# A Mamba-2 and pooling block on one core: where the later adaLN product-sums stand, and in which order the first weights are cast

## The chip, the core and the metric

The kernel runs on one core of a Trainium2 chip. The time is the device time in microseconds (us) of one execution. The engines are TensorE (PE in the profile, with PEld for its weight loads), VectorE (DVE), ScalarE (ACT), GpSimd (POOL) and SyncE (SP), which here issues nearly all transfers. Each engine works its own instructions off in order and waits on semaphores for the others.

## What is computed

One decoder block for 512 tokens of width 1024, in float32. A vector `c` gives six rows of 1024 numbers (shift, scale and gate of each of two sub-layers), and these modulate everything else:

```
mod = silu(c) @ w_ada + b_ada            # 6 x 1024 numbers
shift_m, scale_m, gate_m, shift_f, scale_f, gate_f = split(mod, 6)
h = rmsnorm(x, norm_mix_w) * (1 + scale_m) + shift_m
z, xbc, dt, u_pool, gate_logits = split(h @ w_in)
y = scan(silu(conv(xbc)), dt) * silu(z)          # Mamba-2, 4 groups of 8 heads
y_ssd  = rmsnorm(y by group) @ w_branch_ssd
y_pool = pool(u_pool) @ w_branch_pool
x = x + gate_m * ((sig(g0) * y_ssd + sig(g1) * y_pool) @ w_out)
h = rmsnorm(x, norm_mlp_w) * (1 + scale_f) + shift_f
x = x + gate_f * (relu(h @ w_up) ** 2 @ w_down)
out = rmsnorm(x, norm_final_w)
```

`mod` is held as 48 columns of 128 numbers: columns 0 to 7 shift_m, 8 to 15 scale_m, 16 to 23 gate_m, 24 to 31 shift_f, 32 to 39 scale_f, 40 to 47 gate_f.

## The kernel before

**Three matmuls for one.** PE multiplies in a rounded float format. To keep float32 precision each operand is split into a high part (a cast on ACT) and a low part (the rest, a subtraction on DVE), and each product is three matmuls: high by high, high by low, low by high (`mm3`, L155 to L157). `split` (L125 cast, L126 subtraction) does this for data.

**Units.** A unit is 128 output rows of a weight matrix by all 512 tokens, 24 matmuls. `load_unit` brings its 512 KB weight block: SP issues the transfer into one of four raw buffers (`RAW`, L140), ACT casts it (L145), DVE subtracts (L146), into two of eight `HL` tiles, so that four units' weights can stand ready. The raw buffer is free again after the subtraction, the `HL` tiles after the unit's last matmul. Each of these pools is handed out in turn, in the order in which the program asks.

**The product-sums.** A column of `mod` isn't made on PE. `ada(j)` takes a raw buffer, SP loads a 512 KB block of the transposed `w_ada` into it (L170), and one DVE instruction multiplies it by the row silu(c) and sums (L171). There are 48. Sixteen (shift_m and scale_m) are needed for the first operand and stand in the first stage. The other 32 are spread over later stages: after each of the eight units of the pooling gate (columns 16 to 23), after each of the eight pooling-branch units (24 to 31), after each of the eight units of the other gate (32 to 39), and eight in the first five units of the output projection (40 to 47).

**The order.** The stages are: the first input units with the modulation of the first operand; the remaining z units of group 0; four groups of the state-space scan; gate units; pooling-branch units; second gate units; output projection and the norm; up and down projections. In the first stage the order of each engine is the program's own (`tc.manual_schedule()`). After it a planner orders each engine's instructions: it plays the program through with estimated durations and gives each engine, whenever it is free, the earliest instruction in the program of those that are ready; weight loads rank ahead of all (`urgent`).

**The first stage.** For each of eight slices `k` of the contraction: DVE makes `t` (L305), ACT adds the shift and writes the operand's high part (L306), DVE its low part (L310). The weights of slice 0 come in two transfers, 256 columns (L274 casts them) and the rest (issued at L293, cast at L308); L278 subtracts for all. L320 are the matmuls of seven units, slice by slice; L314 those of the step sizes.

**A group of the scan** (`ssd_group`) works on four chunks of 128 tokens. `prepare(c)` loads decay rows (`cs_d`, L482), masks them on POOL (L487), takes exponentials on ACT (L491), multiplies on DVE (L492), transposes x on PE (L495), and scales it by the step size (L497); for the first three chunks it also scales by the decay on POOL (L503) and splits that for the state's matmul. A chunk then computes the state (three matmuls of `mm3`), the old state's share (L521), and the chunk's own (L541). `run(g, fillers)` gives the program alternately a step of group g and some units of PE work: units of the next group (B, C, four x, four z units: `u_z`, whose result goes to `sz` at L431), or the branch units (`bs`) of the group before. L578 is the norm's sum at a group's end.

**The output projection** does five of its eight units whole, and units 5 to 7 in two halves of 256 tokens each. `residual` (L751) adds a unit to x, squares it (L758), sums the squares (L759), and `norm` (L768) adds them up over the partitions, once for each half. The `wup` blocks of the next stage are loaded meanwhile (L974, L976) and split by `two` (L828, L829).

Of the kernel before, what the change touches and what calls it, by code (L numbers as in the profile page):

```python
# [9 lines left out]
AF = mybir.ActivationFunctionType  # L10
# [52 lines left out]
def block_kernel(tc, xp, crow, arow, par, adaT, wstart, wz, wx, wpool_in, wgate, wpw, wbs, wbp, wout, wup, wdn, out):  # L63
# [3 lines left out]
    with (  # L67
# [99 lines left out]
        def ada(j, at=RAW):  # L167
# [3 lines left out]
            dve.tensor_tensor_reduce(r, r, cbc, 1.0, col("b_ada", j), ALU.mult, ALU.add, mod[:, j:j + 1])  # L171
            at.put(r)

        def column_sums(ps, sqs, c0, c1, opened=False):

            if len(sqs) == 1 and not opened:
                for c in range(c0, c1):
                    pe.matmul(ps[:, c:c + 1], sqs[0][:, c * P:(c + 1) * P], ones[:, :1], start=True, stop=True)
                return
            if not opened:  # L180
                pe.matmul(ps[:, c0:c1], ones, zeros[:, c0:c1], start=True, stop=False)
            for i, sq in enumerate(sqs):
                for c in range(c0, c1):
                    pe.matmul(ps[:, c:c + 1], sq[:, c * P:(c + 1) * P], ones[:, :1], start=False,
                              stop=i == len(sqs) - 1 and c == c1 - 1)
# [32 lines left out]
        with tc.manual_schedule():  # L218
            raw0 = RAW.get()
            crow_t = raw0[:1]  # L220
            act.dma_start(crow_t, crow)
            mt = [MT.get() for _ in range(3)]
            xs1 = HL.get()
            xpair = [m.rearrange("p h k -> p (h k)") for m in mt] + [xs1]
            xs0 = [xpair[k // 2][:, k % 2 * T:k % 2 * T + T] for k in range(8)]
            for i in range(4):
                sp.dma_start(xpair[i], xp[i])
            sp.dma_start(par_t, par)
            warm(12)
            wide = HL.get()  # L230
            dve.memset(wide, 0.0)
            act.activation(wide[:1], crow_t, AF.Silu)
            cps = [PU.get(), PU.get()]
            for i in range(2):
                pe.matmul(cps[i], ones, wide[:, i * T:(i + 1) * T], start=True, stop=True)
            HL.put(wide)
            ps = PU.get()
            sq = [HL.get() for _ in range(4)]

            def halves(i):  # L240
                dve.tensor_tensor(sq[i][:, :T], sq[i][:, :T], sq[i][:, T:], ALU.add)

            def sums(i):
                pe.matmul(ps, ones, sq[i][:, :T], start=i == 1, stop=i == 3)

            for i in range(3):
                act.activation(sq[i], xpair[i], AF.Square)
                halves(i)
                if i == 1:
                    dve.tensor_tensor(sq[1][:, :T], sq[1][:, :T], sq[0][:, :T], ALU.add)  # L250
            act.copy(cbc[:, :T], cps[0])
            act.activation(sq[3][:, :T], xpair[3][:, :T], AF.Square)
            act.copy(cbc[:, T:], cps[1])
            act.preload_act_table_set("natural_log_exp_and_others")
            dve.tensor_tensor(sq[3][:, T:], xpair[3][:, T:], xpair[3][:, T:], ALU.mult)
            halves(3)
            for i in range(1, 4):
                sums(i)
            warm(5)
            PU.put(*cps)  # L260
            RAW.put(raw0)
            HL.put(*sq)

            def scale(k):
                act.activation(amod[:, k:k + 1], mod[:, 8 + k:9 + k], AF.Identity,
                               bias=col("nmix", k), scale=col("nmix", k))

            W0 = NU * P + NH

            def begin(k, n=W0):  # L270

                r, hi, lo = RAW.get(), HL.get(F32R), HL.get(F32R)
                sp.dma_start(r[:, :n], wstart[k][:, :n])
                act.copy(hi[:, :n], r[:, :n])  # L274
                return r, hi, lo

            def end(r, hi, lo):
                dve.tensor_tensor(lo[:, :W0], r[:, :W0], hi[:, :W0].bitcast(F32), ALU.subtract)  # L278
                pool.tensor_copy(hi[:, W0:W0 + NH], lo[:, W0 - NH:W0].bitcast(F32))
                RAW.put(r)  # L280
                HL.put(hi, lo)
                return [(hi[:, o:o + n], lo[:, o:o + n]) for o, n in [(NU * P, 2 * NH)] + [(o, P) for o in range(0, NU * P, P)]]

            h = []
            ada(8, EARLY)
            w = begin(0, 2 * P)
            R = S.get()
            act.activation(R, ps, AF.Ln, bias=eps_t, scale=1.0 / DM)
            act.activation(R, R, AF.Exp, scale=-0.5)
            PU.put(ps)  # L290
            dve.tensor_scalar(amod[:, :1], mod[:, 8:9], 1.0, col("nmix"), ALU.add, ALU.mult)
            ada(0, EARLY)
            sp.dma_start(w[0][:, 2 * P:W0], wstart[0][:, 2 * P:])  # L293
            first = [PS.get() for _ in range(8 - NPU)] + [PU.get() for _ in range(NPU)]
            for k in range(8):
                hi, lo = S.get(F32R), S.get(F32R)
                h.append((hi, lo))
                t = S.get()
                shift = mod[:, k:k + 1]
                if k:  # L300
                    w = begin(k)
                    ada(8 + k, EARLY)
                    scale(k)
                    ada(k, EARLY)
                dve.scalar_tensor_tensor(t, xs0[k], amod[:, k:k + 1], R, ALU.mult, ALU.mult)  # L305
                act.activation(hi, t, AF.Identity, bias=shift)  # L306
                if k == 0:
                    act.copy(w[1][:, 2 * P:W0], w[0][:, 2 * P:W0])  # L308
                w = end(*w)
                dve.scalar_tensor_tensor(lo, t, shift, hi.bitcast(F32), ALU.add, ALU.subtract)  # L310
                S.put(t)
                def dt_unit():
                    for i in range(2):
                        pe.matmul(first[0][:2 * NH], w[0][0], h[k][i], start=k == 0 and i == 0, stop=k == 7 and i == 1)  # L314

                for i in range(3):
                    if k == 7 and i == 2:
                        dt_unit()
                    for u in range(1, NU + 1):
                        pe.matmul(first[u], w[u][i // 2], h[k][i % 2], start=k == 0 and i == 0, stop=k == 7 and i == 2)  # L320
                if k < 7:
                    dt_unit()
            sp.dma_start(ea, arow[0:1, :].broadcast_to([P, NH]))
            act.activation(ea, ea, AF.Exp)
# [101 lines left out]
        def u_z(g, i):  # L426
            def f():
                if "sz" not in G[g]:
                    G[g]["sz"] = SZ.get()
                ps = unit(wz[4 * g + i], h)  # L430
                with tc.issue_after(act.activation(G[g]["sz"][:, i, :], ps, AF.Silu).ins):  # L431
                    silus()
                PU.put(ps)
            return f

        acc = [None] * 8
# [20 lines left out]
        def ssd_group(g):  # L457
# [20 lines left out]
            def prepare(c):  # L478
# [22 lines left out]
                if c < 3:  # L501
                    t = S.get()
                    pool.tensor_tensor(  # L503
                        v3(t), v3(xdt), decg[:, c, :].unsqueeze(2).broadcast_to([P, HG, 64]), ALU.mult)
                    xd = split(t)
                    S.put(t)
                return m, xdt, xd

            ready = [prepare(0)]
            yield  # L510
            for c in range(NC):
                cc = slice(c * P, (c + 1) * P)
                if c < NC - 1:
                    ready.append(prepare(c + 1))
                    yield
                m, xdt, xd = ready.pop(0)
                yo = None
                if c > 0:
                    yo = PS.get()
# [172 lines left out]
        for j in range(8):  # L692
            gp = F.get()
            ps = unit(wgate[8 + j], h)
            behind(act.activation(gp, ps, AF.Sigmoid))
            PU.put(ps)
            merged.append(gp)
            if j == 1:
                for _ in rest:
                    pass  # L700
                later.append(SZ.get())
                F.free += range(12, 16)
                PU.free += PS.free
            if j == 3:
                for i in range(4):
                    bs(3, i)()
                pool_mix(1)()
            ada(16 + j)
        for j in range(8):
            ps = unit(wbp[j], pout)  # L710
            dve.tensor_tensor(merged[j], merged[j], ps, ALU.mult)
            PU.put(ps)
            ada(24 + j)
        free(pout)
        mg = []
        for j in range(8):
# [7 lines left out]
            F.put(merged[j])  # L724
            mg.append(split(gs))
            F.put(gs)
            with tc.issue_after(done[0].ins):
                ada(32 + j)
        free(h)
        with tc.issue_after(last.ins):  # L730
            table = act.preload_act_table_set("natural_log_exp_and_others")
# [42 lines left out]
        for j in range(5):  # L774
            ps = unit(wout[j], mg)
            residual(ps, j, 16)
            PU.put(ps)
            ada(40 + j)
            if j > 1:
                ada(43 + j)  # L780
        for k in range(8):
            dve.tensor_scalar(
                amod[:, 8 + k:9 + k], mod[:, 32 + k:33 + k], 1.0, col("nmlp", k), ALU.add, ALU.mult)
# [405 lines left out]
```

## Time and profile before

| | us |
|---|---|
| median of 3 runs | 967.26 (966.17 to 967.54) |
| profiled execution | 968.35 |
| its span, first to last instruction | 966.6 |

The windows view splits the span. These are busy us in each stretch, and what the transfers moved:

| stretch | what runs there | PE | DVE | ACT | GB/s |
|---|---|---|---|---|---|
| 0 to 60 | first input units | 54.77 | 48.59 | 30.83 | 295 |
| 60 to 132 | group 0 | 71.38 | 61.65 | 65.31 | 144 |
| 132 to 312 | groups 1 and 2 | 179.77 | 123.93 | 110.82 | 114 |
| 312 to 426 | group 3 | 114.00 | 88.34 | 56.80 | 113 |
| 426 to 560 | gate, branch, second gate units | 134.00 | 81.96 | 43.96 | 175 |
| 560 to 624 | end of those, output projection, norm | 61.19 | 52.10 | 28.11 | 203 |
| 624 to 966.6 | up and down projections, end | 334.83 | 202.46 | 163.34 | 91 |

The row of groups 1 and 2 adds two stretches of the view. A busy PE isn't a PE at its peak, as matmuls overlap; what tells is the time in which it stands idle, and what it waits for.

### The profile page before, as it was taken

How to read it: one execution, taken by the hardware profiler on the slowest of the kernel's cores; microseconds unless marked ns; L12 is line 12 of the kernel's file. 1: busy time of each engine (PE TensorE's matmuls, PEld its weight loads, DVE VectorE, ACT ScalarE, POOL GpSimd, SP SyncE). 2: the span in 40 equal slices, each digit the busy share in tenths (PEclk: the TensorE clock that was granted, in tenths of full speed). 3: DMA queues.
4: the chain of work that ended last, by engine and by line, in shares of the span. 5: the costliest groups of instructions: out<-in, count | busy, mean ns of one | idle time of the engine just before them, and what ended most of it. 6: DMA issues, size and time to landing. Idle time of an engine off the chain costs nothing.

```text
span 966.6 us, 13246 instructions
## 1 busy us (share of the span) xinstructions
PE 949.9 (98%) x5131; PEld 803.6 (83%) x5131; DVE 659.0 (68%) x961; ACT 499.2 (52%) x811; POOL 89.7 (9%) x91
## 2 busy tenths in 40 slices
PE   7999999999999999999999999999999999999996
PEld 4877888888888888888888888998899889889986
DVE  7978869467866787978533897895557556664533
ACT  5479975667528542663312334684157127425632
POOL 0102321220312132300000000000000000000000
PEclk9999999999999999999999999999999999999999
DMA  9746333433253334338632687442144225214002
GB/s 369 293 134 178 121 111 120 131 110 109 77 157 110 101 102 131 131 101 254 211 106 90 214 273 241 140 146 69 52 142 132 66 74 166 88 33 153 23 1 87
DMA packets 61761, 129.22 MB, mean 134 GB/s; under 512 B 4673, under 2 KB 29505, under 8 KB 61698
## 3 DMA queue, kind: packets, MB, share of 16 engines
q1 hardware_dynamic: 61696, 128.38, 41.6%
q8 instruction: 40, 0.66, 0.3%
q14 instruction: 23, 0.19, 0.1%
q10 hardware_dynamic: 2, 0.00, 0.0%
HBM read 126.13 MB, written 2.23 MB: 133 GB/s over the span
## 4 chain that ended last, share of the span: by engine, by line
PE 86%; DVE 5%; DMA 4%; ACT 2%; issue 1%; POOL 0%; SPq 0%; DVEq 0%; ACTq 0%; POOLq 0%
PE ps L155 22%; PE ps L156 22%; PE ps L157 22%; PE ps L887 12%; PE ps L320 4%; DMA d<-cs_d 2%; PE ps L541 2%; DMA d<-wout 1%; PE ps L521 1%; DVE d L171 1%; DMA d<-wstart 1%; DVE d L146 1%; DVE s L389 1%; PE ps L495 1%; DMA d<-wup 1%
## 5 line engine op out<-in xcount | busy, mean ns | idle before, releaser
L155 PE MATMUL ps<-s,d 128*128 128x512 f32 (+1 forms) x1080 | 412.2, 382 | 1.8 <-ACT d L145 1.0
L156 PE MATMUL ps<-s,d 128*128 128x512 f32 (+1 forms) x1080 | 408.1, 378 | 0.0
L157 PE MATMUL ps<-s,d 128*128 128x512 f32 (+1 forms) x1080 | 408.1, 378 | 0.0
L155 PEld LDWEIGHTS ps<-s,d 128*128 128x128 f32 x1080 | 202.7, 188 | 42.7 <-issue 2.4
L157 PEld LDWEIGHTS ps<-s,d 128*128 128x128 f32 x1080 | 202.7, 188 | 38.5 <-DVE d L146 0.3
L156 PEld LDWEIGHTS ps<-s,d 128*128 128x128 f32 x1080 | 202.9, 188 | 37.0 <-DVE s L126 0.2
L145 ACT CAST d<-d 128x1024 fp32r<-128x1024 f32 x88 | 92.0, 1046 | 126.6 <-PE ps L156 109.5
L146 DVE TENSOR_TENSOR d<-d,d 128x1024 fp32r<-128x1024 f32 x88 | 112.6, 1280 | 65.6 <-ACT d L145 60.8
L887 PE MATMUL ps<-s,d 128*128 128x256 f32 x864 | 103.8, 279 | 0.0
L887 PEld LDWEIGHTS ps<-s,d 128*128 128x128 f32 x864 | 102.9, 188 | 0.2
L828 ACT CAST d<-d 128x1024 fp32r<-128x1024 f32 x44 | 45.8, 1049 | 79.3 <-PE ps L156 62.8
L1076 DVE SCALAR_TENSOR_TENSOR xs<-ps,mod,xs 128x512 f32<-128x512 f32 x29 | 21.7, 750 | 69.7 <-PE ps L157 69.7
L828 ACT CAST d<-sz 128x1024 fp32r<-128x1024 f32 x32 | 33.7, 1052 | 68.8 <-PE ps L156 48.9
L829 DVE TENSOR_TENSOR d<-d,d 128x1024 fp32r<-128x1024 f32 x44 | 53.5, 1223 | 22.3 <-ACT d L828 20.8
L829 DVE TENSOR_TENSOR d<-sz,d 128x1024 fp32r<-128x1024 f32 x32 | 39.2, 1224 | 19.8 <-ACT d L828 16.5
L171 DVE CUSTOM_DVE_ANT_0 d<-d,d,par_t 128x1024 f32<-128x1024 f32 x32 | 41.6, 1305 | 8.2 <-DMA d<-adaT 8.2
L320 PE MATMUL ps<-s,d 128*128 128x512 f32 x168 | 40.7, 394 | 2.3 <-ACT s L306 1.9
L491 ACT ACTIVATE d<-d,ncs 128x128 f32<-128x128 f32 x128 | 39.9, 391 | 3.6 <-POOL d L487 3.6
L320 PEld LDWEIGHTS ps<-s,d 128*128 128x128 f32 x168 | 31.2, 188 | 10.9 <-ACT s L306 2.8
L389 DVE SCALAR_TENSOR_TENSOR s<-ps,par_t,s 128x511 f32<-128x511 f32 (+2 forms) x54 | 39.6, 740 | 0.3
L125 ACT CAST s<-s 128x512 fp32r<-128x512 f32 x32 | 19.7, 619 | 23.8 <-POOL s L503 18.7
L126 DVE TENSOR_TENSOR s<-s,s 128x512 fp32r<-128x512 f32 x32 | 27.4, 858 | 4.5 <-ACT s L125 4.5
(219 smaller groups left out, 1000.0 us busy)
## 6 DMA issues: line engine op xcount, KB each, us to landing
d<-adaT SPq DMA_DIRECT2D x32, 512.0 KB, 4.2
d<-wx SPq DMA_DIRECT2D x18, 512.0 KB, 3.6
d<-wdn SPq DMA_DIRECT2D x18, 512.0 KB, 4.0
d<-cs_d SPq DMA_DIRECT2D x16, 512.0 KB, 6.1
d<-wbs SPq DMA_DIRECT2D x16, 512.0 KB, 3.5
d<-wgate SPq DMA_DIRECT2D x16, 512.0 KB, 3.6
d<-wz SPq DMA_DIRECT2D x15, 512.0 KB, 3.5
sz<-wdn SPq DMA_DIRECT2D x14, 512.0 KB, 4.0
```

The lines of the kernel that those rows point to most:

```text
L145: act.copy(hi[:, :w], r[:, a:a + w])
L146: (low or dve).tensor_tensor(lo[:, :w], r[:, a:a + w], hi[:, :w].bitcast(F32), ALU.subtract)
L155: pe.matmul(ps, whi, xhi[:, t0:t1], start=start, stop=False)
L156: pe.matmul(ps, whi, xlo[:, t0:t1], start=False, stop=False)
L157: pe.matmul(ps, wlo, xhi[:, t0:t1], start=False, stop=stop)
L171: dve.tensor_tensor_reduce(r, r, cbc, 1.0, col("b_ada", j), ALU.mult, ALU.add, mod[:, j:j + 1])
L320: pe.matmul(first[u], w[u][i // 2], h[k][i % 2], start=k == 0 and i == 0, stop=k == 7 and i == 2)
L389: dve.scalar_tensor_tensor(t[:, sh:], ps[:, :T - sh], w(3 - sh), t[:, sh:], ALU.mult, ALU.add)
L491: act.activation(m[:, i, :], m[:, i, :], AF.Exp, bias=ncs[:, c, g * HG + i:g * HG + i + 1])
L828: act.copy(dst[0], src)
L829: dve.tensor_tensor(dst[1], src, dst[0].bitcast(F32), ALU.subtract)
L887: pe.matmul(ps, x, y, start=start and m == 0 and i == 0, stop=m == 3 and i == 2, skip_group_check=True)
```

## The change

1. `ada_next` hands out the 32 later product-sums in order, columns 16 to 47. One follows each z unit of groups 1 to 3 (12; these units run as fillers of groups 0 to 2), one each of the eight pooling-gate units and the four branch units `bs(3, i)` among them (12), and one each of the eight pooling-branch units (8). The second gate units and the output projection have none.
2. In slice 0 of the first stage, ACT casts the rest of the first weights before it writes the operand's high part, not after.
3. The split of the decay-scaled x leaves `prepare(c)`. It is asked for at the beginning of chunk c, ahead of `prepare(c + 1)`.

```diff
+        rows = list(range(16, 48))
+
+        def ada_next(n=1):
+
+            for _ in range(n):
+                ada(rows.pop(0))
...
                 dve.scalar_tensor_tensor(t, xs0[k], amod[:, k:k + 1], R, ALU.mult, ALU.mult)
-                act.activation(hi, t, AF.Identity, bias=shift)
                 if k == 0:
                     act.copy(w[1][:, 2 * P:W0], w[0][:, 2 * P:W0])
+                act.activation(hi, t, AF.Identity, bias=shift)
...
                 with tc.issue_after(act.activation(G[g]["sz"][:, i, :], ps, AF.Silu).ins):
                     silus()
                 PU.put(ps)
+                if g:
+                    ada_next()
...
-                    xd = split(t)
-                    S.put(t)
+                    xd = t
                 return m, xdt, xd
...
                 cc = slice(c * P, (c + 1) * P)
+                m, xdt, xd = ready.pop(0)
                 if c < NC - 1:
+                    t, xd = xd, split(xd)
+                    S.put(t)
                     ready.append(prepare(c + 1))
                     yield
-                m, xdt, xd = ready.pop(0)
...
+            ada_next()
             if j == 3:
                 for i in range(4):
                     bs(3, i)()
+                    ada_next()
                 pool_mix(1)()
-            ada(16 + j)
...
             PU.put(ps)
-            ada(24 + j)
+            if rows:
+                ada_next()
...
-            with tc.issue_after(done[0].ins):
-                ada(32 + j)
...
             residual(ps, j, 16)
             PU.put(ps)
-            ada(40 + j)
-            if j > 1:
-                ada(43 + j)
```

## The prediction

> **What bounds the kernel now.** I read the page first.
>
> ```profile
> span 966.6 us, 13246 instructions
> PE 949.9 (98%) x5131; PEld 803.6 (83%) x5131; DVE 659.0 (68%) x961; ACT 499.2 (52%) x811; POOL 89.7 (9%) x91
> ```
>
> TensorE (PE) is busy for 98% of the span and its matmuls don't change. So only the places where PE stands still can be won or lost. The view of waits, for PE alone, lists them (waited-for instruction, us in total, times, longest):
>
> ```profile
> PE ps L320 <- ACT s L306: 1.9, 1, 1.9
> PE ps L768 <- DVE sz L759: 1.6, 1, 1.6
> ...
> PE ps L155 <- ACT d L145: 1.0, 1, 1.0
> ...
> PE ps L155 <- ACT sz L431: 0.4, 1, 0.4
> PE ps L320 <- DVE s L310: 0.4, 1, 0.4
> PE ps L578 <- DVE s L126: 0.2, 1, 0.2
> ```
>
> The L320 waits are in the first input units. L145 and L768 are at the output projection, where later product-sums now sit. L431 and L578 are the only waits in the state-space groups. The view by windows gives the engines' load in the stretches of groups 0, 1 and 2 (columns: stretch, its length, busy us of PE, PE weight load, DVE, ACT, POOL, then clock, DMA share, GB/s):
>
> ```profile
> 60.00:132.00 72.00, 71.38 (x381) 57.39 (x380) 61.65 (x105) 65.31 (x124) 19.36 (x19) 1.00 0.47 144
> 132.00:222.00 90.00, 89.77 (x463) 73.59 (x462) 60.54 (x86) 59.87 (x111) 18.47 (x19) 1.00 0.39 114
> 222.00:312.00 90.00, 90.00 (x466) 74.24 (x465) 63.39 (x93) 50.95 (x91) 17.44 (x17) 1.00 0.39 114
> ```
>
> VectorE (DVE) has 10.35 us free in the first (72.00 less 61.65), 29.5 in the second, 26.6 in the third. The clock is full.
>
> **Part 1, the first weights.** From the timeline of the start, and one piece of the chain of waits (the DMA of the first weights' rest):
>
> ```profile
> 4.87 7.60 DMA d<-wstart
> ```
>
> ```profile
> 14.36 0.72 ACT L306 ACTIVATE s<-s,mod 128x512 fp32r<-128x512 f32 x1 [0.82 <-DVE s L305]
> 14.98 0.74 ACT L308 CAST d<-d 128x672 fp32r<-128x672 f32 x1
> 15.13 2.08 PE L320 MATMUL ps<-s,d 128*128 128x512 f32 x7 [1.90 <-ACT s L306]
> 15.76 1.12 DVE L278 TENSOR_TENSOR d<-d,d 128x928 fp32r<-128x928 f32 x1 [1.44 <-ACT d L308]
> 16.80 0.74 DVE L310 SCALAR_TENSOR_TENSOR s<-s,mod,s 128x512 fp32r<-128x512 f32 x1
> 17.60 3.45 PE L320 MATMUL ps<-s,d 128*128 128x512 f32 x14 [0.39 <-DVE s L310]
> 20.65 0.73 ACT L306 ACTIVATE s<-s,mod 128x512 fp32r<-128x512 f32 x1 [1.48 <-DVE s L305]
> 21.43 2.83 PE L320 MATMUL ps<-s,d 128*128 128x512 f32 x11
> ```
>
> The rest has landed at 12.47, and ScalarE (ACT) stands idle for 0.82 us before L306 at 14.36. The cast L308 (0.74) fits into that gap: 13.54 to 14.28, so L306 isn't pushed back. L278 then starts when DVE is done with L305, at 14.3 instead of 15.76, and L310 ends near 16.1 instead of 17.54. PE has all its high weights at 15.13, does its 7 matmuls without a break at some 0.24 us each (3.45 over 14) until 16.75, and goes on at once where it now goes on at 17.60: **-0.85 us**. It lasts if the next operand comes as much earlier. That one (L306 at 20.65) ends with DVE's work, which moves by 1.4, and needs two more rows:
>
> ```profile
> 7.10 1.61 SPq L170 DMA_DIRECT2D xs<-adaT  x2
> ```
>
> ```profile
> xs<-adaT SPq DMA_DIRECT2D x8, 512.0 KB, 7.8
> ```
>
> Issued by 8.7 and 7.8 us to landing, the second operand of its product-sums is there near 16.5, before DVE gets to it (16.1 plus one product-sum). So the next operand is ready near 20.0, and PE, done at 20.6, doesn't wait. Bounds: 0 if one of these transfers is later, -0.9.
>
> **Part 2, what goes away at the output projection.** The chain of waits there (start, us, what):
>
> ```profile
> 578.89 1.14 DVE d L171
> 580.13 5.80 DMA d<-wout
> 585.95 1.05 ACT d L145
> ...
> 599.74 5.05 DMA d<-wup
> 604.82 1.06 ACT d L828
> 605.90 1.23 DVE d L829
> 607.46 0.41 DVE xs L751
> 607.88 0.42 ACT sz L758
> 608.33 0.44 DVE sz L759
> 608.81 0.71 PE ps L768 x2
> ```
>
> A product-sum (L171) gives its raw buffer back, only then is `wout`'s block issued, it lands 5.8 us later, and its cast L145 is what PE waited 1.0 us for. After the change no product-sum stands between these loads: a load waits for the subtraction four loads earlier, which lies some 20 us back. **-1.0**; bounds 0 and -1.0.
>
> The second wait has the same root. The sum for the norm (L751, L758, L759, then L768) runs 607.46 to 608.81, 1.35 us. L751 stood behind L829 on DVE, and that behind a `wup` block which landed at 604.8. When could it have started? The window from 596.75 to 606.85 shows
>
> ```profile
> 596.75:606.85 10.10, 10.10 (x85) 10.06 (x85) 7.74 (x12) 5.35 (x8) 0.00 (x0) 1.00 0.77 238
> ```
>
> 85 matmuls: 72 are the first halves of units 5 to 7 (three units of 24), one is the end of the unit before, 12 are of the second halves, put ahead of the norm. At 10.10/85 = 0.12 each these 12 take 1.4 us, so unit 7 was ready near 605.4 and the norm's matmul could start at 606.9, when PE ran dry. With `wup` loaded earlier DVE is free at 605.4 and the 1.6 us go, all but 0.1: **-1.5**. Bounds: 0 if another thing is in DVE's way, -1.6. What is late next: the norm's own chain, which the 12 matmuls just cover.
>
> **Part 3, what the groups take on.** Twelve product-sums go into the z units of groups 1 to 3, which run during groups 0 to 2, four in each. Each is one 512 KB transfer on SP's queue, one of four raw buffers, and one DVE instruction. The rows of that line, DVE's wait for it, and one case beside GpSimd (POOL):
>
> ```profile
> L171 DVE CUSTOM_DVE_ANT_0 d<-d,d,par_t x32: 1253/1280/2089, 379.2 to 592.0; 128x1024 f32<-128x1024 f32 x32
> ```
>
> ```profile
> DVE d L171 <- DMA d<-adaT: 8.2, 9, 2.0
> ```
>
> ```profile
> 394.86 1.06 POOL L623 TENSOR_TENSOR pad<-pad 128x527 f32<-128x527 f32 x1 [2.84 <-DVE s L627]
> ```
>
> Four in a stretch are 5.1 us of DVE (4 times 1.28): they fit into 29.5 and 26.6 with ease, into group 0's 10.35 just. The dearest one took 2.09, and the POOL addition at 394.86 ran in that time. The Trainium skill (SBUF — State Buffer, Who interferes with whom) says that a VectorE instruction with both inputs in SBUF and a GpSimd instruction that reads SBUF shut each other out; the trace agrees by that one case, and by this rule four of them would cost group 0 up to 3.2 us more of DVE, still inside its free time.
>
> While a product-sum waits for its transfer (2.0 at the longest), what stands behind it on DVE waits too: weight subtractions, convolutions, the scan's operands; PE reads those. Weights are up to four units ahead of PE (eight tiles, two each). The scan is nearer: in group 0
>
> ```profile
> 111.92 0.94 DVE L126 TENSOR_TENSOR s<-s,s 128x512 fp32r<-128x512 f32 x1
> ```
>
> ```profile
> 113.89 0.48 PE L155 MATMUL ps<-s,s 128*128 128x512 f32 x1
> ```
>
> the state operand's low part ended at 112.86, only 1.03 us before PE took it. On SP's queue a transfer that waits for its raw buffer holds up the decay rows (`cs_d`) and other weights behind it. Bounds: -0.6 (the L431 and L578 waits vanish) to 5.1 (group 0's four all on PE's path). The nearest row is the waits view, where all groups cost PE 0.6 with DVE at 86% in group 0; I double it: **+0.6**.
>
> The moved split (ACT cast, DVE subtraction; same count) removes ACT's stops behind POOL:
>
> ```profile
> ACT s L125 <- POOL s L503: 18.7, 7, 4.1
> ```
>
> No PE wait hangs on these, so 0. In exchange the operand is made one filler later; if the 1.03 us above are used up, it costs what is missing, a subtraction (0.94) or so; this lies inside the bound.
>
> The gate stage's twelve (eight before) and the eight in the branch units stay at 0. The window of the gate, branch and second gate units up to 560 shows PE without a gap beside the sums there now, and DVE with a third of its time free:
>
> ```profile
> 426.00:560.00 134.00, 134.00 (x593) 111.00 (x592) 81.96 (x111) 43.96 (x55) 0.00 (x0) 1.00 0.55 175
> ```
>
> **The sum.** -0.85 - 1.0 - 1.5 + 0.6 = -2.75. The profiled execution took 968.35 (span 966.6, 1.75 around it), which would become 965.6; it is 1.1 above the median of the runs, 967.26, and from the median the sum gives **964.5**. About 0.2%, 1.9 us, is what a measurement of this kernel can tell from no change.
>
> **The rivals.** *The norm still waits*: DVE is held by other `wup` subtractions, or the planner puts fewer matmuls ahead of the norm. For it: wait and chain are only 1.4 us apart. Against: the chain names the late transfer. -0.85 - 1.0 + 0.6 = -1.25, 966.0; no measurable change.
>
> *It doesn't do what it says*: the planner, which orders by buffer and readiness, lets the sums drift back to where the raw buffers are free, as it drew three of the gate stage's forward (their line starts at 379.2, before that stage). Then only part 1 is left: 966.4.
>
> *Group 0 becomes the bound*, which makes it slower: four product-sums stand in DVE's queue ahead of the scan's operands. Priced with the dearest row, 4 times 2.09 = 8.4 on PE's path instead of 0.6: -3.35 + 8.4 = +5.0, 972.3. It decides from the point where a sum and its wait take more than the 1.03 us of slack before L155 in group 0; a sum alone is 1.28. For it: DVE at 86% and ACT at 91% there. Against: later chunks of groups 1 and 2 show no PE wait, and a late sum's order is below the scan's own work.
>
> **How the numbers follow.** Forecast 0.55, the norm still waits 0.19, drift 0.09, group 0 bound 0.17. The first is faster by over 0.2%, the next two lie within, the last is slower. The low end takes every bound at its best: -0.9 - 1.0 - 1.6 - 0.6 = -4.1, and 0.6 for small waits beside these: 962.5. The high end takes in the first two rivals and the mild part of the third, 967.9; what is left out is most of the third.
>
> **What would show it.** Part 1: the second L320 row starts near 16.75 and PE's wait there is gone. Part 2: no L171 after 520, `wout` transfers issued well before PE needs them, no PE wait on L145, that on L759 under 0.3. Part 3: PE waits between 60 and 312 near 1.2, no new one on L126, L492 or L404. Wrong if PE's waits in group 0 exceed 3 us, or if sums still run after 560.

## The result, and the profile after

| | median us | lowest to highest | runs |
|---|---|---|---|
| before, measured beside it | 966.35 | 966.12 to 967.54 | 6 |
| changed | 973.04 | 971.21 to 975.12 | 6 |

The ratio is 1.0067, with an interval of 1.0053 to 1.0080. The change makes the kernel slower by 6.7 us; forecast was 964.5. The profiled execution of the changed kernel took 971.21 us, the lowest of its six, and that of the kernel before 968.35, longer than any of the six beside it. So the two profiles understate the loss: their spans are 969.5 and 966.6 us, 2.9 apart. From the page (the span, then busy us of the engines):

```profile
span 969.5 us, 13257 instructions
PE 951.2 (98%) x5131; PEld 804.4 (83%) x5131; DVE 656.2 (68%) x961; ACT 507.1 (52%) x817; POOL 94.2 (10%) x91
```

PE's work and DVE's instructions are as many as before. As before, the view of waits for PE tells where it stood still (us in total, times, longest). In the groups the changed kernel's lines are 7 to 10 higher than before: the norm matmul of a group, L578, is now L588, the convolution L389 is L396.

```profile
PE ps L588 <- ACT s L125: 2.3, 1, 2.3
PE ps L327 <- ACT s L315: 1.9, 1, 1.9
PE ps L156 <- DVE s L126: 1.5, 2, 1.3
...
PE ps L155 <- ACT s L458: 0.8, 1, 0.8
PE ps L155 <- ACT s L651: 0.6, 1, 0.6
```

The waits on L145 and L759 at the output projection are gone, as forecast. New are L588 and L156 (in group 0), L458 (at 174.9, in group 1) and L651 (before the gate stage). In the windows view, PE was busy for 28.95, 20.35 and 7.88 us in the three stretches from 560 to 620 before; after the change it has no gap there (two of the three rows):

```profile
560.00:590.00 30.00, 30.00 (x133) 24.43 (x132) 18.71 (x26) 14.73 (x21) 0.00 (x0) 1.00 0.56 191
590.00:612.00 22.00, 22.00 (x139) 19.84 (x137) 11.42 (x16) 6.31 (x9) 0.00 (x0) 1.00 0.31 96
...
```

**By stage.** PE issues 5131 matmuls in every kernel here, so the start of the nth, as a measure of progress, can be compared between two traces. The table gives how much longer (+) each stretch took than in the profile of before. Each column is one execution. Its first row also holds differences between launches of over 1 us, and in e5 and e6 a stretch at half clock (last section).

| stretch of before, us | changed | split back (e1) | cast alone (e3) | sums in gate and bs (e4) | sums in branch (e5) | four in group 0 (e6) | order kept (e9) | split alone (e10) | changed, order kept (e11) |
|---|---|---|---|---|---|---|---|---|---|
| 1 to 19, first weights | -1.27 | -1.41 | -1.50 | -0.31 | +1.43 | +1.13 | -0.15 | -1.51 | -1.49 |
| 97 to 118, group 0's scan | +1.33 | -0.45 | -0.19 | -0.45 | +0.03 | -0.45 | -0.45 | +2.40 | +1.34 |
| 124 to 138, end of group 0 | +3.82 | +3.90 | -0.09 | +0.08 | +0.03 | +3.52 | -0.65 | -0.49 | -0.65 |
| 150 to 232, group 1 | +1.09 | +1.12 | 0 | 0 | 0 | +1.09 | +2.45 | +0.02 | +2.10 |
| 396 to 442, before and in the gate stage | +1.75 | +1.79 | 0 | +3.82 | 0 | 0 | 0 | 0 | +1.73 |
| 564 to 614, output projection, norm | -3.21 | -3.18 | -0.41 | -3.22 | -2.34 | -2.39 | -2.90 | -3.01 | -3.21 |

The gains came, and three losses outweigh them: two in group 0, one around the gate stage. The largest is the end of group 0, and the timeline there shows its course (start, us, engine, line, operation; in brackets the idle time before it and what ended it). First, for comparison, ACT and POOL of the kernel before:

```profile
125.18 0.63 ACT L564 ACTIVATE s<-sz 128x512 f32<-128x512 f32 x1
...
130.31 0.63 ACT L564 ACTIVATE s<-sz 128x512 f32<-128x512 f32 x1 [0.20 <-DVE sz L563]
...
134.23 0.62 ACT L125 CAST s<-s 128x512 fp32r<-128x512 f32 x1 [1.68 <-POOL s L566]
```

```profile
131.02 0.74 POOL L565 TENSOR_TENSOR s<-s 128x256 f32<-128x256 f32 x1 [3.16 <-ACT s L564]
131.72 1.09 POOL L487 TENSOR_SCALAR_AFFINE_SELECT d<-d 128x1024 f32<-128x1024 f32 x1
132.78 1.42 POOL L566 TENSOR_TENSOR s<-s 128x128 f32<-128x128 f32 x1
```

Then DVE and ACT of the changed kernel:

```profile
121.37 1.27 DVE L171 CUSTOM_DVE_ANT_0 d<-d,d,par_t 128x1024 f32<-128x1024 f32 x1
...
127.59 1.29 DVE L573 TENSOR_TENSOR sz<-s,sz 128x512 f32<-128x512 f32 x2
```

```profile
129.97 0.22 ACT L493 ACTIVATE cd<-d 128x8 f32<-128x8 f32 x1 [6.31 <-DMA d<-cs_d]
130.09 0.62 ACT L574 ACTIVATE s<-sz 128x512 f32<-128x512 f32 x1
...
131.55 0.63 ACT L574 ACTIVATE s<-sz 128x512 f32<-128x512 f32 x1
...
136.31 0.62 ACT L125 CAST s<-s 128x512 fp32r<-128x512 f32 x1 [1.18 <-POOL s L576]
```

and POOL:

```profile
131.61 0.46 POOL L576 TENSOR_TENSOR s<-s 128x128 f32<-128x128 f32 x1
132.03 2.08 POOL L496 TENSOR_SCALAR_AFFINE_SELECT d<-d 128x1024 f32<-128x1024 f32 x1
134.08 0.73 POOL L575 TENSOR_TENSOR s<-s 128x256 f32<-128x256 f32 x1
134.77 1.09 POOL L496 TENSOR_SCALAR_AFFINE_SELECT d<-d 128x1024 f32<-128x1024 f32 x1
135.83 0.45 POOL L576 TENSOR_TENSOR s<-s 128x128 f32<-128x128 f32 x1
```

In the changed kernel DVE does a product-sum (L171) at 121.37, and both last chunks' gated outputs (L573) come together at 127.59; before, the first came at 124.01. ACT then has group 1's first decay exponential (L493) ahead of group 0's two squares (L574) in its queue, and that waits for a transfer of decay rows until 129.97. POOL adds up the squares (L575, L576) but has group 1's masks (L496, 2.08 and 1.09 us) between them; before, only the mask of 1.09 stood between the last two additions. So the norm's operand L125 is cast at 136.31, and PE, which waits for it and its subtraction, starts L588 at 136.98. Then it costs once more. The windows, one us each (the number after POOL's is the granted clock):

```profile
137.00:138.00 1.00, 0.82 (x2) 0.46 (x3) 1.00 (x2) 1.00 (x4) 0.00 (x0) 0.65 0.00 0
138.00:139.00 1.00, 1.00 (x3) 0.81 (x3) 1.00 (x3) 1.00 (x4) 0.49 (x1) 0.50 0.00 0
...
140.00:141.00 1.00, 1.00 (x4) 0.85 (x3) 0.70 (x1) 0.99 (x2) 0.00 (x0) 0.65 0.00 0
141.00:142.00 1.00, 1.00 (x6) 0.80 (x5) 0.00 (x0) 1.00 (x3) 0.00 (x0) 1.00 0.75 74
```

After the idle 2.34 us the clock is 0.50 for a while: three or four matmuls a us instead of six.

### The profile page after: what moved, and what is told of

It reads as the page before. It is cut to its first block, busy times and chain, and to the rows that moved or that the text cites. A ratio compares the mean times of both kernels' runs of the same rounds, so it can differ in the third digit from the quotient of the medians.

```text
span 969.5 us, 13257 instructions
## 1 busy us (share of the span) xinstructions
PE 951.2 (98%) x5131; PEld 804.4 (83%) x5131; DVE 656.2 (68%) x961; ACT 507.1 (52%) x817; POOL 94.2 (10%) x91
## 4 chain that ended last, share of the span: by engine, by line
PE 74%; DVE 6%; ACT 4%; issue 1%; POOL 0%; DVEq 0%; ACTq 0%; POOLq 0%
PE ps L155 20%; PE ps L156 20%; PE ps L157 20%; PE ps L894 12%; DVE s L126 1%; DVE d L146 1%; PE ps L551 1%; DVE pad L633 1%; DVE d L171 1%; PE ps L531 1%; ACT d L145 1%; PE ps L504 0%; ACT s L125 0%; DVE s L637 0%; ACT d L500 0%
## 5 line engine op out<-in xcount | busy, mean ns | idle before, releaser
L156 PE MATMUL ps<-s,d 128*128 128x512 f32 (+1 forms) x1080 | 408.8, 379 | 0.2 <-DVE s L126 0.2
L156 PEld LDWEIGHTS ps<-s,d 128*128 128x128 f32 x1080 | 203.1, 188 | 37.6 <-DVE s L126 0.7
L145 ACT CAST d<-d 128x1024 fp32r<-128x1024 f32 x88 | 92.0, 1045 | 109.2 <-PE ps L156 95.7
L171 DVE CUSTOM_DVE_ANT_0 d<-d,d,par_t 128x1024 f32<-128x1024 f32 x32 | 42.2, 1318 | 18.4 <-DMA d<-adaT 18.4
L396 DVE SCALAR_TENSOR_TENSOR s<-ps,par_t,s 128x511 f32<-128x511 f32 (+2 forms) x54 | 39.9, 742 | 0.2
L125 ACT CAST s<-s 128x512 fp32r<-128x512 f32 x32 | 19.7, 618 | 26.3 <-POOL s L512 14.4
L126 DVE TENSOR_TENSOR s<-s,s 128x512 fp32r<-128x512 f32 x32 | 25.0, 783 | 10.0 <-ACT s L125 10.0
```

The source lines that it names most:

```text
L145: act.copy(hi[:, :w], r[:, a:a + w])
L156: pe.matmul(ps, whi, xlo[:, t0:t1], start=False, stop=False)
L396: dve.scalar_tensor_tensor(t[:, sh:], ps[:, :T - sh], w(3 - sh), t[:, sh:], ALU.mult, ALU.add)
```

## The experiments

All medians, with the ratio to the kernel before run beside each. Rows are compared by these ratios where a difference is small, as the kernel before itself had medians from 966.35 to 967.64 beside them:

| run | median us | ratio, 95% |
|---|---|---|
| changed | 973.04 | 1.0067 [1.0053, 1.0080] |
| e1 split back in `prepare` | 972.57 | 1.0049 [1.0030, 1.0067] |
| e2 no sums in the z units | 971.35 | 1.0040 [1.0027, 1.0052] |
| e3 earlier cast alone | 966.68 | 1.0000 [0.9989, 1.0011] |
| e4 cast, 24 sums in gate and `bs` units | 968.37 | 1.0008 [0.9999, 1.0017] |
| e5 cast, sums in gate and branch units | 964.83 | 0.9973 [0.9963, 0.9984] |
| e6 as e5, four sums in group 0 | 968.88 | 1.0023 [1.0011, 1.0034] |
| e7 as e5, four extra transfers | 965.67 (one run) | |
| e8 as e5, four extra sums without transfer | 965.3 (one run) | |
| e9 as e6, ACT's order kept | 966.56 | 0.9991 [0.9977, 1.0005] |
| e10 as e5, split moved | 966.89 | 0.9992 [0.9980, 1.0003] |
| e11 changed, ACT's order kept | 968.73 | 1.0011 [0.9996, 1.0025] |
| e12 as e5, ACT's order kept | 967.83 | 1.0006 [0.9993, 1.0019] |

**e1 and e2: one part of the changed kernel undone.** Theory S blames the moved split, theory Z the sums in the z units.

```diff
e1:
-                    xd = t
+                    xd = split(t)
+                    S.put(t)
...
-                    t, xd = xd, split(xd)
-                    S.put(t)
...
e2:
-                if g:
-                    ada_next()
...
-            ada_next()
+            ada_next(2)
...
-                    ada_next()
+                    ada_next(2)
```

> The changed kernel with the split of the decay-scaled x put back into prepare. Theory S (the moved split): the 1.3 us wait of the state's matmul at 113 us goes, and the wait at the end of group 0 (2.3 us and the low clock behind it) falls below 1; some 968. Theory Z (the sums in the z units): both waits at the end of group 0 stay, 971 to 973.

> The changed kernel without sums in the z units: their twelve go as second sums to the twelve gate and branch units. Theory Z: the group stretches are as before, 964. Theory S: the wait at 113 us and the long one at the end of group 0 stay, 969 or more.

e1 took back the 1.3 us at 97 to 118 and nothing at the end of group 0 (+3.90). Its 972.57 is within what theory Z expected. e2 took the end of group 0 back (-0.52 there), but its 24 sums in the gate and `bs` units brought 3.8 us instead of 1.75 at 396 to 442, so that theory Z's 964 was missed by 7 us (971.35). Each theory holds for its own stretch, and neither undoing brings the gain back.

**e3 and e4: the gains by themselves.** e3 is the kernel before with the earlier cast alone; e4 is the changed kernel with the edits of both e1 and e2.

```diff
e3, from before:
-                act.activation(hi, t, AF.Identity, bias=shift)
                 if k == 0:
                     act.copy(w[1][:, 2 * P:W0], w[0][:, 2 * P:W0])
+                act.activation(hi, t, AF.Identity, bias=shift)
```

> The kernel before, with the earlier cast of the first weights alone. Both theories: 0.85 us less than before, 965.5, if what follows lets the gain pass; a theory that the end of group 0 is set by its own chain and not by TensorE: the gain is eaten there, 966.3.

> The changed kernel with both undone: split back in prepare, the z units' sums as second sums of the gate and branch units. What is left is the earlier cast and an output projection free of sums. Both theories: 0.85 + 1.0 + 1.5 less than before, 963.

e3's 966.68 is above both expectations. The cast alone can't be told from no change by its median; its interval just holds the 0.85 us that the timeline gives it, and nothing is eaten at the end of group 0 (-0.09). e4 missed its 963 by 5 us (968.37): it has the whole gain at the output projection and loses it around the gate stage, where it has 24 sums, so these aren't free. In the changed kernel (12 there) the first such place, in DVE's and PE's timeline:

```profile
398.42 1.28 DVE L171 CUSTOM_DVE_ANT_0 d<-d,d,par_t 128x1024 f32<-128x1024 f32 x1
...
400.70 0.68 DVE L637 SCALAR_TENSOR_TENSOR s<-pad,pad 128x512 f32<-128x512 f32 x1
401.30 1.28 DVE L171 CUSTOM_DVE_ANT_0 d<-d,d,par_t 128x1024 f32<-128x1024 f32 x1
```

```profile
402.67 0.50 PE L155 MATMUL ps<-s,d 128*128 128x512 f32 x1 [0.62 <-ACT s L651]
```

Sums stand before the pooling operand (L637) and before what follows it; ACT's L651, which PE waits for, comes later. About half of the 1.75 us arises there (0.93). The rest, and 2.9 us in e4, arises at 432 to 436, at group 3's normed operand. In e4 two product-sums stand among its splits on DVE, and PE waits for these (0.77, 0.49 and 0.65 us). In the changed kernel none stands there; the operand's scaling starts at 433.14, against 425.94 before, 1.7 us more than the kernel's own lag of 5.5 us there. Which of the earlier sums delays it isn't shown.

**e5 and e6: a place without loss, and then only four sums moved to group 0.** e5 starts from the kernel before, with the earlier cast; its sums stand behind the gate units (8), the branch units (two each) and the second gate units (8), none at the output projection or in the groups. e6 moves four of the branch units' sums to group 0.

```diff
e5, from before:
-            ada(24 + j)
+            ada(24 + 2 * j)
+            ada(25 + 2 * j)
...
-                ada(32 + j)
+                ada(40 + j)
...
-            ada(40 + j)
-            if j > 1:
-                ada(43 + j)
e6, from e5, in u_z:
                 PU.put(ps)
+                if g == 1:
+                    ada(24 + i)
... and in the branch units:
-            ada(24 + 2 * j)
-            ada(25 + 2 * j)
+            ada(28 + j)
+            if j > 3:
+                ada(32 + j)
```

> The earlier cast, the split where it was, and no sum in the groups or at the output projection: eight in the gate units and eight in the second gate units as before, sixteen (two each) in the branch units. Theory Z, widened (a sum costs where VectorE's results are near the next use on TensorE, in the groups and the gate units, and nothing where a unit's time is its own): the stretches 120 to 175 and 396 to 442 us are as before, the output projection keeps its 3.2 us gain, some 963. Rival (sums cost about the same wherever they stand, the late stages only hide them): new waits in the branch units, 965 or more.

> The kernel of e5 with four of the branch units' second sums moved into the z units of group 1, which run during group 0. Theory Z: these four alone bring back the 3.9 us at the end of group 0 (124 to 138 us), with the low clock after the wait: some 967. Rival (it takes all twelve, or the moved split): under 1 us there, 963 to 964.

e5 beats both kernels, 2.6 us under before by its ratio. Its 964.83 lies between the two expectations; PE loses nothing around the gate stage (0.00 at 396 to 442). Its profiled execution (967.16) was the longest of its ten. Four sums in group 0 cost 4.05 us of median (968.88 less 964.83; 4.8 by the ratios; theory Z said 3.9), and the profile puts them where the changed kernel has them: +3.52 at the end of group 0, +1.09 behind. ACT's queue in e5, and then in e6 (squares L564 and L566, decay exponentials L484 and L486):

```profile
126.43 0.63 ACT L564 ACTIVATE s<-sz 128x512 f32<-128x512 f32 x1
...
131.02 0.22 ACT L484 ACTIVATE cd<-d 128x8 f32<-128x8 f32 x1 [0.95 <-DMA d<-cs_d]
131.55 0.63 ACT L564 ACTIVATE s<-sz 128x512 f32<-128x512 f32 x1 [0.31 <-DVE sz L563]
```

```profile
130.31 0.22 ACT L486 ACTIVATE cd<-d 128x8 f32<-128x8 f32 x1 [6.72 <-DMA d<-cs_d]
130.43 0.62 ACT L566 ACTIVATE s<-sz 128x512 f32<-128x512 f32 x1
...
131.89 0.63 ACT L566 ACTIVATE s<-sz 128x512 f32<-128x512 f32 x1
```

The transfer arrives at nearly the same time in both. In e5 one square is done before that wait, so that only the last is left, which waits for DVE's gated output (L563); in e6 both stand behind it. PE in e5 runs 1.13 us behind e6 at this point (the start of the matmul at 122). With that taken off, e6's last square ends 1.5 us later than e5's and POOL's last addition 2.3 us later (136.61 against 135.44): an estimate of how the delay divides, some 1.5 us by ACT's order and 0.8 by POOL's masks.

**e7 and e8: the transfers or DVE's work alone.** e7 is e5 with four extra transfers of 512 KB into a raw buffer that nothing reads; e8 is e5 with four extra DVE sums of the same length over data that lie there already, their results unused, each with a raw buffer taken and given back.

```diff
e7:
+                if g == 1:
+                    r = RAW.get()
+                    sp.dma_start(r, adaT[24 + i])
+                    RAW.put(r)
e8:
+                if g == 1:
+                    r = RAW.get()
+                    dve.tensor_tensor_reduce(r, cbc, cbc, 1.0, col("b_ada", 24), ALU.mult, ALU.add, junk)
+                    RAW.put(r)
```

> The kernel of e5 with four more transfers of a product-sum's size in the z units of group 1, each with its raw buffer and nothing on VectorE. If the transfers, their buffers and SyncE's queue are what delays the end of group 0: 2 to 4 us more at 124 to 138 us. If it is VectorE's instruction: none.

> The kernel of e5 with four more product-sums on VectorE in the z units of group 1, of data that lie ready, so without a transfer or a wait for one; each still takes a raw buffer. If VectorE's time (four times 1.28 us) delays the end of group 0: 2 to 4 us more at 124 to 138 us. If it is the wait for the transfer: under 1.

At 124 to 174 the transfers cost -0.66 and the DVE work about 1.0 (0.73 + 0.30), against 5.05 (3.52 + 0.44 + 1.09) for both together in e6. The transfers did bring one new wait earlier: at 90.34 PE waited 1.13 us for the state's operand; by 174 e7 had made it up (-0.29 from 19 to 174, against -0.20 in e5). So the DMA load isn't the price, and DVE's time is about a fifth of it, by one execution each. By its recorded words e8's result speaks for a sum's wait for its transfer; but in e6 no product-sum of group 0 stood waiting for one. In e8 a square still goes ahead of the wait for the decay rows. This led to the theory of the order.

**e9 and e11: the order alone.** Nothing is taken out; ACT gets group 1's decay exponentials only behind group 0's last square.

```diff
-                    act.activation(cdg[:, c, :], m[:, :, P - 1], AF.Exp)
+                    with tc.issue_after(G[0]["sq"].ins) if g == 1 else nullcontext():
+                        act.activation(cdg[:, c, :], m[:, :, P - 1], AF.Exp)
...
-                    act.activation(v4(y), sz[:, :, cc], AF.Square)
+                    G[g]["sq"] = act.activation(v4(y), sz[:, :, cc], AF.Square)
```

> The kernel with four sums in group 0 (968.9), with one thing changed: ScalarE takes group 1's decay exponentials (which wait for a transfer) only after the last square of group 0. In its order POOL's two sums of squares then also stand ahead of group 1's mask. All the added instructions of the sums stay. Theory 'order': most of the 4.05 us that the four sums cost came from the two squares queueing behind that wait, and from the half clock that the idle TensorE brought; then the stretch 123.6-138.0 is within 0.9 us of the kernel without these sums, TensorE waits under 1 us for group 0's normalising sum, no half clock at 137-141, and the time is 965.0 to 966.8. Rival 'VectorE's time': the 4 x 1.28 us of sums ahead of the last operands cost what they last wherever the squares stand; the time stays at 968 to 969.5.

> The changed kernel (973.0) with group 1's decay exponentials put after group 0's last square on ScalarE, nothing else. Theory 'order': 3 to 3.8 us come back at 123.6-141, as in the small case, the 1.8 us of the moved split and the 1.7 us of the gate stage stay: 969.2 to 970.3. Rival 'VectorE's time': 972.5 to 973.5.

Both speak for the order theory. e9 (966.56) came out as it said: 3.1 us under e6 by the ratios (0.9991 and 1.0023), no wait for the norm's sum, no half clock there. e11 gained more than it said: 968.73, under its range of 969.2 to 970.3, 4.5 us less at 124 to 138 and 5.4 us under the changed kernel by the ratios (1.0011 and 1.0067). DVE's late outputs stayed (e11's first square starts at 128.04, e9's at 127.83), so they weren't the price. In e11's POOL timeline no mask stands between the sums:

```profile
128.76 0.74 POOL L576 TENSOR_TENSOR s<-s 128x256 f32<-128x256 f32 x1 [13.92 <-ACT s L575]
...
130.42 1.57 POOL L576 TENSOR_TENSOR s<-s 128x256 f32<-128x256 f32 x1 [0.38 <-ACT s L575]
132.07 0.46 POOL L577 TENSOR_TENSOR s<-s 128x128 f32<-128x128 f32 x1
134.78 4.16 POOL L497 TENSOR_SCALAR_AFFINE_SELECT d<-d 128x1024 f32<-128x1024 f32 x3 [2.25 <-ACT cd L494]
```

The norm's sum is ready at 132.5 instead of 136.3, and e11's PE waits from 95 to 180 show what stays above all, the split:

```profile
PE ps L156 <- DVE s L126: 2.3, 2, 1.2
```

The edit moves more than the squares: group 1's decay and masks come later too, and e9 and e11 lose 1.0 to 1.4 us more than e6 and the changed kernel at 150 to 232. How much of the gain is ACT's order and how much POOL's, these two runs don't tell apart.

**e10: the split alone, on e5.**

```diff
-                    xd = split(t)
-                    S.put(t)
+                    xd = t
...
+                m, xdt, xd = ready.pop(0)
                 if c < NC - 1:
+                    t, xd = xd, split(xd)
+                    S.put(t)
                     ready.append(prepare(c + 1))
...
```

> The fastest version so far (964.8: earlier cast, sums in the gate and branch units) with the scan's split moved as in the change, and nothing else. Theory 'split': the move costs by itself because VectorE's half of the split stands behind the next chunk's convolutions; 1.3 to 1.9 us more at 97-118, none elsewhere; 966.1 to 966.8. Rival: the move costs only together with sums in VectorE's queue; 964.3 to 965.4.

1.8 us by the ratios (0.9992 and 0.9973; their intervals are 0.001 wide to each side), +2.40 in the profile at 97 to 118, with no sum in the groups: theory 'split', a little above both its figures. DVE of the kernel before, then of e10, and PE of e10:

```profile
112.78 4.01 DVE L389 SCALAR_TENSOR_TENSOR s<-ps,par_t,s 128x511 f32<-128x511 f32 x6
```

```profile
109.79 1.51 DVE L146 TENSOR_TENSOR d<-d,d 128x1024 fp32r<-128x1024 f32 x1
111.23 4.01 DVE L389 SCALAR_TENSOR_TENSOR s<-ps,par_t,s 128x511 f32<-128x511 f32 x6
115.17 0.67 DVE L126 TENSOR_TENSOR s<-s,s 128x512 fp32r<-128x512 f32 x1
```

```profile
115.90 0.50 PE L156 MATMUL ps<-s,s 128*128 128x512 f32 x1 [1.44 <-DVE s L126]
```

Before the change L126 (111.92, shown in the prediction) stood ahead of these convolutions (L389, from 112.78). Now six of them, 4.01 us, go first, though ACT's half of the split was done at 110.6 (L125 at 109.97, 0.61).

**e12: the order on the fastest version.** The edit of e9 on e5.

> The fastest version so far (964.8) with group 1's decay exponentials put after group 0's last square. There TensorE has no wait of more than 0.2 us at the end of group 0, so theory 'order' (the order costs only where it makes TensorE idle) expects no gain: 964.2 to 965.8. Rival: the order is worth something by itself, by taking waits off ScalarE and POOL; under 964.0.

Both expectations missed: 967.83, 3 us slower than e5. The end of group 0 is 0.65 us shorter, but the stretch 150 to 174 takes 3.27 more. ACT's exponentials for group 1 now come later, and ACT changes activation tables four times from 163.75 to 172.24 (1.28 us each), where e5 does so once from 155 to 182; that this causes the waits is argued, not tested. The first two of PE's waits from 90 to 330:

```profile
PE ps L155 <- ACT s L449: 1.8, 1, 1.8
PE ps L155 <- DVE s L389: 0.9, 1, 0.9
```

The order was worth something only where PE stood idle for it, and here it moved work to a place where PE then waited.

## Why the prediction was wrong

- **Part 1 (-0.85): right in place.** PE's first 21 matmuls of L320 took from 15.13 to 21.05, with the stop at 17.60; now they are one row of 5.05 us without a stop, 0.87 less. Between 14 and 20 us ten of the thirteen kernels with the earlier cast are 0.82 to 0.87 us faster than before; in e5, e6 and e7 half clock turns this into 0.73 or 0.74 us slower (last section). The median of e3 doesn't show the gain.
- **Part 2 (-1.0 and -1.5): right, a little small.** Both waits are gone, no product-sum runs after 484, and the stretch is 3.2 us shorter, for 2.5 forecast. With Part 1 the forecast was -3.35; e5, which has these two parts and no new loss in the groups or the gate stage, is 2.6 us faster (1.5 to 3.6).
- **Part 3, the groups (+0.6): the step that failed.** It took the present waits of 0.6 us, doubled, as the price, and held DVE's free time against the sums' length. That test was the wrong one: DVE's time was cheap (e8, about 1.0 us), the order was not. e6 shows 4.05 us for group 0's four sums alone (4.8 by the ratios), and e9 that most of it (3.1) is the order on ACT and POOL, squares behind a transfer's wait and sums behind masks, with the clock after it. The prediction did see that a late transfer holds up what stands behind it, but looked at DVE's queue and SP's alone.
- **Part 3, the moved split (0, "this lies inside the bound"): wrong, 1.8 us.** The step did name the row: the operand had 1.03 us before PE took it. It didn't ask what would stand ahead of L126 in DVE's queue after the move; it is six convolutions.
- **Part 3, the gate stage (0): wrong, 1.75 us in the profile.** The window it was read from begins at 426 and is an average up to 560, while in the changed kernel sums stand more densely in the pooling work from 398 on. The window there in the kernel before shows DVE busy for 19.45 of 20 us, so here DVE's time was scarce:

```profile
392.00:412.00 20.00, 20.00 (x90) 16.57 (x89) 19.45 (x30) 12.56 (x19) 3.57 (x4) 1.00 0.37 132
```

- The rival **"Group 0 becomes the bound"** (0.17) is what happened: 972.3 against 973.04. Its own sign held, PE waits in group 0 over 3 us (2.3 + 1.3 + 0.2). But that its price came so near is luck: it put 8.4 us of sums on PE's path, where four sums cost about half of that, not by their length, and the split and the gate stage most of the rest. The clash that the prediction weighed from the Trainium skill (SBUF — State Buffer, Who interferes with whom) played next to no part: group 0's four sums took 1.28, 1.40, 1.28 and 1.27 us, where it would have allowed 3.2 us more.

From e5's ratio, four sums in group 0 (+0.0050), the split (+0.0019) and the gate stage's 1.75 us (+0.0018) make 1.0060, of 1.0067. This leaves out that in the profiles the output projection gains 0.9 us more in the changed kernel than in e5, so up to 1.6 us of its loss has no place here. The eight sums of groups 1 and 2 cost nothing that can be seen (0.00 us from 174 to 396 in the changed kernel's profile).

Open stays why the planner, given the four sums, put the exponential ahead of the square: the traces show the order, and that the first square's input came 3.6 us later from DVE, not the reason.

## What to carry to other kernels

Spare time on an engine is no price for work put on it: look at which instruction on the path stands behind the new one in its queue, and what else the queue's order then changes on the other engines. Look above all for an instruction that waits for a transfer and stands ahead of work on the critical path; an edit that takes it away is worth only what the bounding engine stood idle for. When one part of a change gains and another loses, try them one by one: here the gain with the sums at a place without loss (e5) beats both kernels.

## What the hardware showed unexpectedly

The clock halves after a short stop, and not every time. In the changed kernel PE was idle for 2.34 us before 136.98 and 0.18 after, and the next matmuls ran at 0.50 until 140.7; PE's timeline gives the spacing:

```profile
138.30 0.63 PE L155 MATMUL ps<-s,d 128*128 128x512 f32 x1
...
140.80 0.39 PE L155 MATMUL ps<-s,d 128*128 128x512 f32 x1
141.03 0.39 PE L156 MATMUL ps<-s,d 128*128 128x512 f32 x1
```

Six intervals from 138.30 to 140.80 take 2.50 us; at 0.23 each they would take 1.4, so these alone cost 1.1. In e12 PE was idle for 1.83 us before 171.78 and the clock stayed at 1.00:

```profile
171.00:172.00 1.00, 0.22 (x1) 0.22 (x2) 1.00 (x1) 1.00 (x3) 1.00 (x1) 1.00 0.00 0
```

The length of the stop doesn't decide alone. In each of the fourteen traces PE waits 1.90 to 1.93 us for the high part of the first operand. In e5, e6 and e7 the clock behind it was 0.50 for some 3.4 us, in the other eleven 1.00. The first 21 matmuls of the changed kernel, and of e5, with a window of e5:

```profile
14.72 5.05 PE L327 MATMUL ps<-s,d 128*128 128x512 f32 x21 [1.92 <-ACT s L315]
```

```profile
15.82 6.66 PE L320 MATMUL ps<-s,d 128*128 128x512 f32 x21 [1.93 <-ACT s L308]
17.00:18.00 1.00, 1.00 (x4) 0.81 (x3) 1.00 (x3) 0.05 (x1) 0.00 (x0) 0.50 1.03 420
```

The same wait thus cost 1.6 us more in some launches than in others, and a profile of one execution has this chance in it.

The Trainium skill (TensorE: Matmul & The Clock Gate, Why this matters for your kernels) advises no idle gaps over about 3 us. Here 2.34 us were enough, and in three traces 1.9, so for this kernel the measurement decides. The Trainium skill (TensorE: Matmul & The Clock Gate, Part 1: The HAM clock gate) says that the activity window is free-running and some 3.4 us long. The half clock here lasted about that, 137.3 to 140.7 by the windows at 0.65 (0.7 us of each at half). A window that runs free of the kernel would also explain why equal stops differ between launches; no run here tests that.

The mean granted clock of the changed kernel's six runs is 0.9945, that of e11's twelve 0.9969, and of the six the one at 0.997 took 971.21 us and the one at 0.992 975.12. That the other executions lose more at the end of group 0 than the profiled one is likely from it, and not shown.
